# Operand tiles of a hybrid decoder block moved to multiples of 512 bytes, its feed-forward transposes spread over the next block, and w_down taken in halves between blocks of w_up

## The chip, the cores and the metric

The kernel runs on one core of a Trainium2 chip. The metric is the device time of one execution in microseconds (us), the median of several runs.

## The reference

One layer of a hybrid decoder block on 256 tokens of width 2048, in float32:

```python
u = rmsnorm(h, norm1_g);  proj = u @ w_in            # HGRN2 q,f,i,g; attention q,k,v; two gates
ya = hgrn2_branch(hq, hf, hi, hg) @ w_proj_a
yb = dilated_attention_branch(aq, ak, av) @ w_proj_b
h = h + (sigmoid(gate_a) * ya + sigmoid(gate_b) * yb) @ w_out
v = rmsnorm(h, norm2_g)
hup = v @ w_up                                       # 2048 x 11264
hc = depthwise causal conv of width 3 over tokens (hup) + conv_b
h = h + (gelu(hc[:, :5632]) * hc[:, 5632:]) @ w_down # 5632 x 2048
return rmsnorm(h, norm_f_g)
```

## The kernel before

All weights (318 MB) pass once through the core, in one stream of units. A unit is 128 x 2048 floats (1 MB): 16 tiles of 128 x 128. `load` (L230) issues its DMA on SP's queue into one of three `raw` buffers. `split` (L288) makes of each half a high part `hi` (a copy by ACT, L306, in the matmul's rounded type) and a low part `lo` (raw minus hi, by DVE, L311), in four buffers each. `begin_unit` (L344) splits two units ahead of the one that PE is at. A float32 product then is three products of PE: low operand with hi, high with hi, high with lo.

In a product the stationary operand is 128 x 128 and the moving one 128 x 512 (or x 256 in part of the first stage). `tile_step` (L374) takes the weights as the stationary operand and the tokens `xu` as the moving one (attention's q and k, HGRN2's q and f). `moving_step` (L459) takes the tokens as the stationary operand and the weights as the moving one: v and out-gate (names `avp`, `vp`, `gp`), gates (`egp`), `yb`, `ya`, `wo`, and w_down (`dn`).

For w_up, `sevenfold` (L508) takes two rows of blocks and two columns of blocks of the weights per unit, into seven banks of PSUM. A unit of mode P is eight block products (24 of PE); a unit of mode S (`split_s`, L262) is seven (21 of PE), with sums of weight blocks (`sa`, `se`, `sf`, `sg`) and sums of token blocks (`hvs`, `hvx`). Mode A is P with another way to the low part of its second half: ACT writes the negated raw (L308), and a DMA of POOL's queue adds raw to it (L309). A block b of w_up is eight units in the modes `SPAPSAPA`; there are eleven blocks. `unfold` (L524) combines the seven banks into four tiles, and `convolved` (L928) transposes them on PE (L936) into side banks and does the convolution with one ACT and two DVE instructions for each 128 columns (L939 to L941). Gelu, a multiplication and the split into `ff` follow. After blocks 3, 6, 9 and 11 (`PARTS`, L34) all of w_down's rows for these blocks pass, for each of four column blocks j. A scheduler sets the order of each engine's instructions from the order in which the program is traced and from the buffers.

Where the tiles lie follows from the pools, one behind the other in each partition. Counted modulo 512 bytes, the tiles of pools `wp` (raw, hi, lo, sa) and `sb` (tag `w4`: ot, ob, ff, hva, hvs, hvx) start at 448. Those of `sbe`, `sbm`, `sbh` and `sbl` (xu, mix, hvd, se, sf, sg) start at 480, since the small tiles at the end of `sb` shift what lies behind them. Every product operand starts at a multiple of 512 bytes within its tile.

Of the kernel before, what the change touches and what calls it, by code (L numbers as in the profile page):

```python
# [11 lines left out]
F32 = mybir.dt.float32  # L12
F32R = mybir.dt.float32r
# [29 lines left out]

START_X = {0: ((2, 4),), 1: ((4, 8),), 2: ((8, 12),), 3: ((12, 16),)}
# [1 line left out]

def up_order(b):

    return (1, 2, 0, 3, 5, 4, 6, 7) if b == 0 else tuple(range(KD // 2))

# [3 lines left out]
def stream_spec():  # L54
    spec, modes = [], {}

    def stat(name, col, k0, nk):
        for k in range(k0, k0 + nk):
            spec.append((name, k * P, col))

    def mov(name, col, k0, nk):
        for k in range(k0, k0 + nk):
            for c in range(4):
                spec.append((name, k * P, col + c * P))

    def pairs(name, n1, n2, k0, modes_of, order):

        for i in order:
            mode = modes_of[i]
            k2, k1 = k0 + 2 * i, k0 + 2 * i + 1  # L70
# [33 lines left out]
    for b0, b1 in PARTS:  # L104
        for b in range(b0, b1):
            pairs("w_up", b * 512, DFF + b * 512, 0, UP_PAIRS, up_order(b))
        for j in range(NJ):
# [59 lines left out]
def hybrid_block(ctx, tc, x_p, x_t, weights, g1, gf, params, c_rope, c_mask0, c_mask1, c_level, out):  # L167
    nc = tc.nc
    vec, act, pe = nc.vector, nc.scalar, nc.tensor

    const = ctx.enter_context(tc.tile_pool(name="const", bufs=1))
    wp = ctx.enter_context(tc.tile_pool(name="wp", bufs=1))
    sb = ctx.enter_context(tc.tile_pool(name="sb", bufs=1))
    early = ExitStack()
    sbe = early.enter_context(tc.tile_pool(name="sbe", bufs=1))
    psm = ctx.enter_context(tc.tile_pool(name="psm", bufs=4, space=bass.MemoryType.PSUM))
    pss = ctx.enter_context(tc.tile_pool(name="pss", bufs=4, space=bass.MemoryType.PSUM))

    def w4(shape, name, dt=F32):
        return sb.tile([P] + list(shape), dt, tag="w4", name=name, bufs=20)  # L180
# [81 lines left out]
    def split_s(u):  # L262
# [7 lines left out]
        q = pool.tile([P, 2, 512], F32, tag="q", name=f"q{u}", bufs=1)  # L270
# [6 lines left out]
        vec.tensor_tensor(r[:, 3], r[:, 3], r[:, 2], op=ALU.add)  # L277
# [5 lines left out]
        splits[u] = {  # L283
            "11": (ah[:, 0], al[:, 0]), "21": (ah[:, 1], al[:, 1]), "22": (eh[:, 0], el[:, 0]),
            "q3": (eh[:, 1], el[:, 1]), "q1": (fh[:, 0], fl[:, 0]), "q2": (fh[:, 1], fl[:, 1]), "q4": (g[:, 0], g[:, 1]),
        }

    def split(u):  # L288
# [8 lines left out]
        for s in range(2):  # L297
# [4 lines left out]
            for q in range(n):  # L302
# [1 line left out]
                if u < KD // 2 and q == 0:  # L304
                    split_x(2 * u + s)
                last[0] = act.activation(hi[:, q * w : (q + 1) * w], raw, AF.Copy)  # L306
                if s and MODES.get(u) == "A":
                    act.activation(lo, raw, AF.Copy, scale=-1.0)  # L308
                    nc.gpsimd.dma_start(lo, raw, accum_op=ALU.add)  # L309
                else:  # L310
                    last[1] = vec.tensor_tensor(lo[:, q * w : (q + 1) * w], raw, hi[:, q * w : (q + 1) * w].bitcast(F32), op=ALU.subtract)  # L311
            parts.append((hi, lo))
        splits[u] = parts

# [150 lines left out]
            pe.matmul(pst[m], xh, hi, start=False, stop=False)  # L465
            pe.matmul(pst[m], xh, lo, start=False, stop=(k == k0 + nk - 1))  # L466

    def moving(parts, k0, nk, name):

        pst = [main_bank(f"{name}_{m}") for m in range(2)]  # L470
        for k in range(k0, k0 + nk):
            moving_step(pst, parts, k, k0, nk)
        return pst
# [8 lines left out]
            (5, "a21", "12"), (5, "a22", "22"), (3, "d1", "12"), (3, "d2", "22"),  # L482
        ),
    }
    PRODUCTS["A"] = PRODUCTS["P"]

    def operands(a, mode, i, name):

# [18 lines left out]

    def sevenfold(ops, modes_of, order, name):  # L508

        banks = {i: (main_bank if i < 5 else side_bank)(f"{name}_{i}") for i in range(1, 8)}  # L510
        left = {i: sum(p[0] == i for mode in modes_of for p in PRODUCTS[mode]) for i in banks}
        fresh = set(banks)
        for i in order:
            w = next_pair()
            for b, x, n in PRODUCTS[modes_of[i]]:
                (xh, xl), (wh, wl) = ops[i][x], w[n]
                left[b] -= 1
                pe.matmul(banks[b], xl, wh, start=b in fresh, stop=False)  # L518
                pe.matmul(banks[b], xh, wh, start=False, stop=False)  # L519
                pe.matmul(banks[b], xh, wl, start=False, stop=left[b] == 0)  # L520
                fresh.discard(b)
        return banks

    def unfold(p, r, name):  # L524

# [396 lines left out]
    rstd2 = rsqrt_tokens(ss2, "rstd2")  # L922

    mid.close()
    late["pool"] = late["stage"] = ctx.enter_context(tc.tile_pool(name="sbl", bufs=1))


    def convolved(ups, c0, name):  # L928

        t = late["pool"].tile([P, FB, T], F32, tag="uc", name=f"{name}c", bufs=2)  # L930
        for i in range(2):
            pt = side_bank(f"{name}t{i}").rearrange("p (c t) -> p c t", c=2)
            for c in range(2):
                for m in range(2):
                    n = (2 * i + c) * P
# [1 line left out]
            for c in range(2):  # L937
# [1 line left out]
                act.activation(d, s, AF.Identity, bias=pc("cb", col), scale=pc("cw2", col))  # L939
                vec.scalar_tensor_tensor(d[:, 1:], s[:, : T - 1], pc("cw1", col), d[:, 1:], op0=ALU.mult, op1=ALU.add)  # L940
                vec.scalar_tensor_tensor(d[:, 2:], s[:, : T - 2], pc("cw0", col), d[:, 2:], op0=ALU.mult, op1=ALU.add)  # L941
        return t

    ss3 = square_sums("ss3")
    for part, (b0, b1) in enumerate(PARTS):
        ff = [w4([2, 2, T], f"ff{part}_{i}", F32R) for i in range((b1 - b0) * FB // 2)]
        for b in range(b0, b1):
            a0, a1, g0, g1_ = unfold(sevenfold(hv, UP_PAIRS, up_order(b), f"up{b}"), rstd2, f"up{b}")
            a = convolved((a0, a1), b * FB, f"ua{b}")
            gelu = act.activation(a, a, AF.Gelu_apprx_tanh)  # L950
            if b == NBLK - 1:

                with in_turn(gelu):
                    act.activation(small([1], "tab", "tab", 1), eps, AF.Sqrt)
            g = convolved((g0, g1_), NFF + b * FB, f"ub{b}")
            vec.tensor_tensor(g, a, g, op=ALU.mult)
            for i in range(2):
                d, s = ff[(b - b0) * 2 + i], g[:, 2 * i : 2 * i + 2]
                act.activation(d[:, :, 0], s, AF.Copy)
                vec.tensor_tensor(d[:, :, 1], s, d[:, :, 0].bitcast(F32), op=ALU.subtract)  # L960

        if b1 == NBLK:
            gfb = [w4([2, 512], f"gfb{i}") for i in range(2)]
            for i in range(2):
                nc.gpsimd.dma_start(gfb[i].rearrange("p a n -> p (a n)"), gf[:, i * 1024 : (i + 1) * 1024].to_broadcast([P, 1024]))

        def ff_parts(k, m, ff=ff, k0=b0 * FB):
            t = ff[(k - k0) // 2][:, (k - k0) % 2]
            return t[:, 0, m * P : (m + 1) * P], t[:, 1, m * P : (m + 1) * P]

        for j in range(NJ):
            pst = moving(ff_parts, b0 * FB, (b1 - b0) * FB, f"dn{part}_{j}")
# [62 lines left out]
```

## Time and profile before

| | |
|---|---|
| median of 3 runs | 1787.72 us (1786.76 to 1787.87) |
| profiled execution | 1786.24 us |
| span of its instructions | 1784.5 us |
| first stage up to w_out, from the first product | 6.4 to 1020.4 us of the span |
| w_up and w_down | 1020.4 to 1772.4 us |
| final norm and output | 1772.4 to 1784.5 us |

PE is TensorE, PEld its weight loads, DVE VectorE, ACT ScalarE, POOL GpSimd and SP SyncE. A matmul's row starts when its operand begins to stream, and ends when its modelled result is out, so that rows overlap: how fast PE goes is read from starts, or from how many products fall into a stretch. A row of a group reads: line, engine, operation, output<-inputs, shape, how many | busy us, mean ns of one | idle time before them and what ended it.

### The profile page before, as it was taken

The numbers are of one execution on the slowest core, as the hardware profiler recorded it, in microseconds if no ns is written. First come the engines' busy times: TensorE is split into PE (matmuls) and PEld (weight loads), VectorE is DVE, ScalarE is ACT, GpSimd is POOL, SyncE is SP. The second block draws the span as 40 slices with busy tenths as digits, with TensorE's granted clock in tenths as the row PEclk, the third lists the DMA queues.
The fourth block names the chain that finished last, engine by engine and source line by source line (L and its number), as shares of the span: only waits on it lengthen the run. The fifth ranks groups of instructions, "written<-read, shape, count | busy, mean of one in ns | idle before, by whom it ended". The sixth has DMA issues, their size and how long they took to land.

```text
span 1784.5 us, 21599 instructions
## 1 busy us (share of the span) xinstructions
PE 1754.5 (98%) x8406; PEld 1453.0 (81%) x8406; DVE 1204.1 (67%) x1499; ACT 951.7 (53%) x1177; POOL 38.3 (2%) x57
## 2 busy tenths in 40 slices
PE   9999999999999999999999999999999999999997
PEld 7888888888888888888887877888787887788775
DVE  7765675867768575445566588766786667776765
ACT  6444565545454545444445567555665456654653
POOL 0000000000000000000000000000000000000000
PEclk9999999999999999999999999999999999999998
DMA  7765644444544444556555576656666566655672
GB/s 271 236 212 201 211 143 154 167 167 166 180 167 169 164 167 160 184 187 236 184 183 189 174 237 212 199 204 206 200 219 214 190 216 224 205 212 201 213 232 85
DMA packets 53126, 345.35 MB, mean 194 GB/s; under 512 B 6128, under 2 KB 6384, under 8 KB 14880
## 3 DMA queue, kind: packets, MB, share of 16 engines
q1 hardware_dynamic: 45648, 318.28, 49.6%
q0 software_dynamic: 6224, 22.55, 6.1%
q10 hardware_dynamic: 1152, 3.15, 0.5%
q8 instruction: 66, 1.08, 0.2%
q14 instruction: 36, 0.29, 0.0%
HBM read 321.41 MB, written 2.10 MB: 181 GB/s over the span
## 4 chain that ended last, share of the span: by engine, by line
PE 89%; DVE 4%; DMA 4%; issue 2%; ACT 1%; SPq 0%; DVEq 0%; POOLq 0%; ACTq 0%
PE up L520 7%; PE up L519 7%; PE up L518 7%; PE dn L464 4%; PE dn L465 4%; PE dn L466 4%; PE egp L464 3%; PE egp L466 3%; PE egp L465 3%; DMA lo<-raw 3%; PE ak L377 2%; PE gp L464 2%; PE gp L466 2%; PE vp L464 2%; PE vp L466 2%
## 5 line engine op out<-in xcount | busy, mean ns | idle before, releaser
L306 ACT ACTIVATE hi<-raw 128x1024 fp32r<-128x1024 f32 (+1 forms) x558 | 588.0, 1056 | 703.1 <-PE dn L465 108.0
L311 DVE TENSOR_TENSOR lo<-raw,hi 128x1024 fp32r<-128x1024 f32 (+1 forms) x525 | 638.8, 1219 | 434.8 <-ACT hi L306 426.4
L520 PE MATMUL up<-lo,hva 128*128 128x512 f32 x396 | 155.5, 393 | 2.7 <-DMA lo<-raw 2.7
L518 PE MATMUL up<-hi,hva 128*128 128x512 f32 x396 | 154.7, 391 | 0.0
L519 PE MATMUL up<-hi,hva 128*128 128x512 f32 x396 | 154.6, 390 | 0.0
L464 PE MATMUL dn<-hi,ff 128*128 128x512 f32 x352 | 138.7, 395 | 2.9 <-DVE ff L960 2.9
L466 PE MATMUL dn<-lo,ff 128*128 128x512 f32 x352 | 137.0, 391 | 1.0 <-DVE lo L311 1.0
L465 PE MATMUL dn<-hi,ff 128*128 128x512 f32 x352 | 137.9, 392 | 0.0
L464 PE MATMUL egp<-hi,xu 128*128 128x512 f32 x256 | 102.1, 399 | 0.0
L466 PE MATMUL egp<-lo,xu 128*128 128x512 f32 x256 | 101.3, 396 | 0.0
L465 PE MATMUL egp<-hi,xu 128*128 128x512 f32 x256 | 101.2, 396 | 0.0
L520 PEld LDWEIGHTS up<-lo,hva 128*128 128x128 f32 x396 | 74.3, 188 | 21.4 <-DMA lo<-raw 5.7
L519 PEld LDWEIGHTS up<-hi,hva 128*128 128x128 f32 x396 | 74.3, 188 | 16.0
L518 PEld LDWEIGHTS up<-hi,hva 128*128 128x128 f32 x396 | 74.4, 188 | 15.9
L464 PEld LDWEIGHTS dn<-hi,ff 128*128 128x128 f32 x352 | 66.5, 189 | 17.7 <-DVE ff L960 4.2
L466 PEld LDWEIGHTS dn<-lo,ff 128*128 128x128 f32 x352 | 66.4, 189 | 15.3 <-DVE lo L311 1.5
L465 PEld LDWEIGHTS dn<-hi,ff 128*128 128x128 f32 x352 | 66.6, 189 | 13.3
L377 PE MATMUL ak<-xu,hi 128*128 128x512 f32 x192 | 66.7, 390 | 0.0
L309 POOL DMA_DIRECT2D lo<-raw x33 | 28.8, 872 | 1491.0 <-ACT lo L308 1360.4
L466 PEld LDWEIGHTS egp<-lo,xu 128*128 128x128 f32 x256 | 48.1, 188 | 11.6
L465 PEld LDWEIGHTS egp<-hi,xu 128*128 128x128 f32 x256 | 48.1, 188 | 11.2
L464 PEld LDWEIGHTS egp<-hi,xu 128*128 128x128 f32 x256 | 48.1, 188 | 11.1
(583 smaller groups left out, 3737.5 us busy)
## 6 DMA issues: line engine op xcount, KB each, us to landing
raw<-weights SPq DMA_DIRECT2D x298, 1024.0 KB, 4.8
lo<-raw POOLq DMA_DIRECT2D x33, 512.0 KB, 5.3
h<-x_t ACTq DMA_DIRECT2D x4, 512.0 KB, 4.5
xt<-x_p SPq DMA_DIRECT2D x3, 512.0 KB, 10.4
xs_q<-aqraw POOLq DMA_DIRECT2D x6, 256.0 KB, 6.6
xs_k<-akraw POOLq DMA_DIRECT2D x6, 256.0 KB, 7.6
raw<-weights SPq DMA_DIRECT2D x4, 256.0 KB, 4.5
raw<-weights SPq DMA_DIRECT2D x2, 512.0 KB, 7.4
```

The source lines that it names most:

```text
L306: last[0] = act.activation(hi[:, q * w : (q + 1) * w], raw, AF.Copy)
L309: nc.gpsimd.dma_start(lo, raw, accum_op=ALU.add)
L311: last[1] = vec.tensor_tensor(lo[:, q * w : (q + 1) * w], raw, hi[:, q * w : (q + 1) * w].bitcast(F32), op=ALU.subtract)
L377: pe.matmul(ps, hi, pair, start=(k == 0), stop=False, skip_group_check=True)
L464: pe.matmul(pst[m], xl, hi, start=(k == k0), stop=False)
L465: pe.matmul(pst[m], xh, hi, start=False, stop=False)
L466: pe.matmul(pst[m], xh, lo, start=False, stop=(k == k0 + nk - 1))
L518: pe.matmul(banks[b], xl, wh, start=b in fresh, stop=False)
L519: pe.matmul(banks[b], xh, wh, start=False, stop=False)
L520: pe.matmul(banks[b], xh, wl, start=False, stop=left[b] == 0)
```

## The change

Three edits.

**Places.** The small tiles get a pool of their own (`smp`) ahead of the others, followed by an unused tile of 136 floats. With it all tiles of `wp`, `sb`, `sbe`, `sbm`, `sbh` and `sbl` start at multiples of 512 bytes. `ones`, `ident` and the other constants stay where they were.

**w_up.** The modes of a block become `SPPSPPPP`: two S and six P as products go, but no A, so the three A halves of a block are split by ACT and DVE as the others are. `split_s` keeps its sums in `raw`'s own blocks, and q1, q2 and q4 change places in the tiles. The seven sums and the transposes get a fixed bank each (`late_bank`; 8 is the transposes').

**Side work.** `hidden_side` is a generator: unfold at the end of a block, then two empty steps, then the convolution's four groups of four transposes, gelu and the split into ff; `begin_unit` takes about one step at each following unit. w_down no longer passes in four parts: from block 2 on, after each block, two column blocks j of the two blocks before that are finished (`DOWN`), eight k tiles each.

```diff
-PARTS = ((0, 3), (3, 6), (6, 9), (9, NBLK))
-UP_PAIRS = "SPAPSAPA"
+DOWN = {b: [(j, b - 2 - b % 2, b - b % 2) for j in ((2, 3) if b % 2 else (0, 1))] for b in range(2, NBLK)}
+DOWN[NBLK - 1] += [(2, NBLK - 3, NBLK), (3, NBLK - 3, NBLK), (0, NBLK - 1, NBLK), (1, NBLK - 1, NBLK)]
+UP_PAIRS = "SPPSPPPP"
+HIDDEN_WAIT = 2
+ALIGN = 136
...
-    return (1, 2, 0, 3, 5, 4, 6, 7) if b == 0 else tuple(range(KD // 2))
+    return (1, 2, 0, 4, 3, 5, 6, 7) if b == 0 else tuple(range(KD // 2))
...
     const = ctx.enter_context(tc.tile_pool(name="const", bufs=1))
+    smp = ctx.enter_context(tc.tile_pool(name="smp", bufs=1))
+    align = ctx.enter_context(tc.tile_pool(name="align", bufs=1))
+    nc.gpsimd.memset(align.tile([P, ALIGN], F32, name="align"), 0.0)
     wp = ctx.enter_context(tc.tile_pool(name="wp", bufs=1))
...
-        return sb.tile([P] + list(shape), F32, tag=tag, name=name, bufs=bufs)
+        return smp.tile([P] + list(shape), F32, tag=tag, name=name, bufs=bufs)
...
-        vec.tensor_tensor(q[:, 0], r[:, 0], r[:, 3], op=ALU.add)
+        vec.tensor_tensor(q1, r[:, 0], r[:, 3], op=ALU.add)
         two_parts(ah, al, r[:, 0:2])
         vec.tensor_tensor(r[:, 3], r[:, 3], r[:, 2], op=ALU.add)
-        vec.tensor_tensor(q[:, 1], q[:, 0], r[:, 2], op=ALU.add)
+        vec.tensor_tensor(r[:, 0], q1, r[:, 2], op=ALU.add)
         two_parts(eh, el, r[:, 2:4])
-        vec.tensor_tensor(r[:, 0], q[:, 1], r[:, 1], op=ALU.add)
-        two_parts(fh, fl, q[:])
-        two_parts(g[:, 0], g[:, 1], r[:, 0])
+        vec.tensor_tensor(r[:, 1], r[:, 1], r[:, 0], op=ALU.add)
+        two_parts(fh, fl, r[:, 0:2])
+        two_parts(g[:, 0], g[:, 1], q1)
...
-                if s and MODES.get(u) == "A":
-                    act.activation(lo, raw, AF.Copy, scale=-1.0)
-                    nc.gpsimd.dma_start(lo, raw, accum_op=ALU.add)
-                else:
-                    last[1] = vec.tensor_tensor(lo[:, q * w : (q + 1) * w], raw, hi[:, q * w : (q + 1) * w].bitcast(F32), op=ALU.subtract)
+                last[1] = vec.tensor_tensor(lo[:, q * w : (q + 1) * w], raw, hi[:, q * w : (q + 1) * w].bitcast(F32), op=ALU.subtract)
...
+    def hidden_side(b, sums):
+        c11, c21, c12, c22 = unfold(sums, rstd2, f"up{b}")
+        for _ in range(HIDDEN_WAIT):
+            yield SIDE_US
+        a, g = (late["pool"].tile([P, FB, T], F32, tag="uc", name=f"u{n}{b}", bufs=2) for n in "ab")
+        yield from convolve((c11, c21), b * FB, a, f"ua{b}")
+        gelu = act.activation(a, a, AF.Gelu_apprx_tanh)
...
+        yield from convolve((c12, c22), NFF + b * FB, g, f"ub{b}")
+        vec.tensor_tensor(g, a, g, op=ALU.mult)
...
+    for b in range(NBLK):
+        sums = sevenfold(hv, UP_PAIRS, up_order(b), f"up{b}")
+        drain()
+        side.append(hidden_side(b, sums))
+        pump(0.0001)
+        for j, b0, b1 in DOWN.get(b, ()):
...
+            pst = moving(ff_parts, b0 * FB, (b1 - b0) * FB, f"dn{b}_{j}", [late_bank(i, f"dn{b}_{j}_{i}") for i in ((4, 3) if j % 2 else (1, 5))])
```

On PE, where block 0 of w_up ends and block 1 begins, before (`ua0t` takes the transposes of block 0's tiles `up0c`; `sah`, `sal` open block 1):

```order
L520 MATMUL up_3_8049<-lo_1_8251,hvd_8017 128x512
L936 MATMUL ua0t_8376<-ident,up0c_8362 128x128
L936 MATMUL ua0t_8387<-ident,up0c_8362 128x128
L518 MATMUL up_1_8427<-sah_8279,hvs_7469 128x512
L519 MATMUL up_1_8427<-sah_8279,hvs_7469 128x512
L520 MATMUL up_1_8427<-sal_8280,hvs_7469 128x512
L518 MATMUL up_2_8428<-sah_8279,hvs_7469 128x512
L519 MATMUL up_2_8428<-sah_8279,hvs_7469 128x512
L520 MATMUL up_2_8428<-sal_8280,hvs_7469 128x512
L518 MATMUL up_2_8428<-hi_0_8324,hva_7485 128x512
L936 MATMUL ua0t_8376<-ident,up0c_8363 128x128
L936 MATMUL ua0t_8376<-ident,up0c_8362 128x128
```

The same place with the change, from the last products of block 1's first unit (an S unit) on:

```order
L523 MATMUL up_5_8383<-sg_8289,hvx_7478 128x512
L521 MATMUL up_3_8381<-seh_8285,hvx_7478 128x512
L522 MATMUL up_3_8381<-seh_8285,hvx_7478 128x512
L523 MATMUL up_3_8381<-sel_8286,hvx_7478 128x512
L945 MATMUL ua0t_8441<-ident,up0c_8366 128x128
L945 MATMUL ua0t_8441<-ident,up0c_8367 128x128
L945 MATMUL ua0t_8441<-ident,up0c_8366 128x128
L945 MATMUL ua0t_8441<-ident,up0c_8367 128x128
L521 MATMUL up_2_8380<-hi_0_8328,hva_7493 128x512
L522 MATMUL up_2_8380<-hi_0_8328,hva_7493 128x512
```

Before, two transposes stand right behind the block's last product and the other fourteen seven products later; now the first four stand a whole unit, 21 products, behind it, and the other twelve in fours further on.

On DVE, after block 0's tiles (`up0c`) are made, before (`ua0c` and `ub0c` are the convolution's results, `lo` a weight unit's low part):

```order
L539 SCALAR_TENSOR_TENSOR up0c_8364<-up_3_8049,rstd_r,up0c_8364 128x512
L311 TENSOR_TENSOR lo_0_8435<-raw_8332,hi_0_8434 128x1024
L940 SCALAR_TENSOR_TENSOR ua0c<-ua0t_8376,par,ua0c 128x255
L940 SCALAR_TENSOR_TENSOR ua0c<-ua0t_8387,par,ua0c 128x255
L941 SCALAR_TENSOR_TENSOR ua0c<-ua0t_8376,par,ua0c 128x254
L941 SCALAR_TENSOR_TENSOR ua0c<-ua0t_8387,par,ua0c 128x254
L940 SCALAR_TENSOR_TENSOR ub0c<-ub0t_8400,par,ub0c 128x255
L940 SCALAR_TENSOR_TENSOR ub0c<-ub0t_8411,par,ub0c 128x255
```

And with the change (`q`, `sg`, `sel`, `sal` belong to the S unit that PE reaches two units later):

```order
L283 TENSOR_TENSOR q_8417<-raw_8394 128x512
L285 TENSOR_TENSOR raw_8394<-raw_8394 128x512
L949 SCALAR_TENSOR_TENSOR ua_8439<-ua0t_8441,par,ua_8439 128x255
L268 TENSOR_TENSOR sg_8424<-q_8417,sg_8424 128x512
L950 SCALAR_TENSOR_TENSOR ua_8439<-ua0t_8441,par,ua_8439 128x254
L268 TENSOR_TENSOR sel_8421<-raw_8394,seh_8420 128x1024
L949 SCALAR_TENSOR_TENSOR ua_8439<-ua0t_8441,par,ua_8439 128x255
L268 TENSOR_TENSOR sal_8419<-raw_8394,sah_8418 128x1024
L950 SCALAR_TENSOR_TENSOR ua_8439<-ua0t_8441,par,ua_8439 128x254
L286 TENSOR_TENSOR raw_8394<-q_8417,raw_8394 128x512
L288 TENSOR_TENSOR raw_8394<-raw_8394 128x512
```

Before, the convolution's instructions stand together; now they alternate with the preparation of the weights.

More of the change, by code (lines that the diff above doesn't have):

```diff
@@ L103, in stream_spec @@
         mov("w_out", j * 512, 0, KD)
[L104 to L107, printed above, removed]
+    for b in range(NBLK):
+        pairs("w_up", b * 512, DFF + b * 512, 0, UP_PAIRS, up_order(b))
+        for j, b0, b1 in DOWN.get(b, ()):
             mov("w_down", j * 512, b0 * FB, (b1 - b0) * FB)
@@ L466, in moving_step, with moving @@
             pe.matmul(pst[m], xh, lo, start=False, stop=(k == k0 + nk - 1))
-    def moving(parts, k0, nk, name):
-        pst = [main_bank(f"{name}_{m}") for m in range(2)]
+    def moving(parts, k0, nk, name, pst=None):
+        pst = pst or [main_bank(f"{name}_{m}") for m in range(2)]
         for k in range(k0, k0 + nk):
@@ L484, in hybrid_block @@
     }
-    PRODUCTS["A"] = PRODUCTS["P"]
     def operands(a, mode, i, name):
@@ L508, in sevenfold @@
     def sevenfold(ops, modes_of, order, name):
-        banks = {i: (main_bank if i < 5 else side_bank)(f"{name}_{i}") for i in range(1, 8)}
-        left = {i: sum(p[0] == i for mode in modes_of for p in PRODUCTS[mode]) for i in banks}
-        fresh = set(banks)
+        sums = {i: late_bank(i, f"{name}_{i}") for i in range(1, 8)}
+        left = {i: sum(p[0] == i for mode in modes_of for p in PRODUCTS[mode]) for i in sums}
+        fresh = set(sums)
         for i in order:
@@ L517, in sevenfold @@
                 left[b] -= 1
-                pe.matmul(banks[b], xl, wh, start=b in fresh, stop=False)
-                pe.matmul(banks[b], xh, wh, start=False, stop=False)
-                pe.matmul(banks[b], xh, wl, start=False, stop=left[b] == 0)
+                pe.matmul(sums[b], xl, wh, start=b in fresh, stop=False)
+                pe.matmul(sums[b], xh, wh, start=False, stop=False)
+                pe.matmul(sums[b], xh, wl, start=False, stop=left[b] == 0)
                 fresh.discard(b)
-        return banks
+        return sums
     def unfold(p, r, name):
@@ L924, in hybrid_block, with late_bank, convolve @@
     mid.close()
+    banks.close()
+    psu = ctx.enter_context(tc.tile_pool(name="psu", bufs=1, space=bass.MemoryType.PSUM))
+    def late_bank(i, name):
+        return psu.tile([P, 512], F32, tag=f"b{i}", name=name)
     late["pool"] = late["stage"] = ctx.enter_context(tc.tile_pool(name="sbl", bufs=1))
-    def convolved(ups, c0, name):
-        t = late["pool"].tile([P, FB, T], F32, tag="uc", name=f"{name}c", bufs=2)
+    def convolve(ups, c0, t, name):
         for i in range(2):
-            pt = side_bank(f"{name}t{i}").rearrange("p (c t) -> p c t", c=2)
+            pt = late_bank(8, f"{name}t{i}").rearrange("p (c t) -> p c t", c=2)
             for c in range(2):
@@ L941, in convolved @@
                 vec.scalar_tensor_tensor(d[:, 2:], s[:, : T - 2], pc("cw0", col), d[:, 2:], op0=ALU.mult, op1=ALU.add)
-        return t
-    ss3 = square_sums("ss3")
[L945 to L972, printed above, removed]
@@ new lines, in convolve @@
+            yield SIDE_US
+    ff = {}
+    def hidden_side(b, sums):
+        c11, c21, c12, c22 = unfold(sums, rstd2, f"up{b}")
+        for _ in range(HIDDEN_WAIT):
+            yield SIDE_US
+        a, g = (late["pool"].tile([P, FB, T], F32, tag="uc", name=f"u{n}{b}", bufs=2) for n in "ab")
+        yield from convolve((c11, c21), b * FB, a, f"ua{b}")
+        gelu = act.activation(a, a, AF.Gelu_apprx_tanh)
+        if b == NBLK - 1:
+            with in_turn(gelu):
+                act.activation(small([1], "tab", "tab", 1), eps, AF.Sqrt)
+        yield from convolve((c12, c22), NFF + b * FB, g, f"ub{b}")
+        vec.tensor_tensor(g, a, g, op=ALU.mult)
+        ff[b] = [w4([2, 2, T], f"ff{b}_{i}", F32R) for i in range(2)]
+        for i in range(2):
+            d, s = ff[b][i], g[:, 2 * i : 2 * i + 2]
+            two_parts(d[:, :, 0], d[:, :, 1], s)
@@ new lines, in ff_parts @@
+    def ff_parts(k, m):
+        t = ff[k // FB][k % FB // 2][:, k % 2]
+        return t[:, 0, m * P : (m + 1) * P], t[:, 1, m * P : (m + 1) * P]
+    gfb = []
+    ss3 = square_sums("ss3")
+    for b in range(NBLK):
+        sums = sevenfold(hv, UP_PAIRS, up_order(b), f"up{b}")
+        drain()
+        side.append(hidden_side(b, sums))
+        pump(0.0001)
+        for j, b0, b1 in DOWN.get(b, ()):
+            if b1 == NBLK and not gfb:
+                drain()
+                for i in range(2):
+                    gfb.append(w4([2, 512], f"gfb{i}"))
+                    nc.gpsimd.dma_start(gfb[i].rearrange("p a n -> p (a n)"), gf[:, i * 1024 : (i + 1) * 1024].to_broadcast([P, 1024]))
+            pst = moving(ff_parts, b0 * FB, (b1 - b0) * FB, f"dn{b}_{j}", [late_bank(i, f"dn{b}_{j}_{i}") for i in ((4, 3) if j % 2 else (1, 5))])
```

10 lines of the change are left out of this document (6 added, 4 removed).

## The prediction

> **What bounds the kernel now.** First the page: busy shares, and the chain of work that ended last.
>
> ```profile
> PE 1754.5 (98%) x8406; PEld 1453.0 (81%) x8406; DVE 1204.1 (67%) x1499; ACT 951.7 (53%) x1177; POOL 38.3 (2%) x57
> ...
> PE 89%; DVE 4%; DMA 4%; issue 2%; ACT 1%; SPq 0%; DVEq 0%; POOLq 0%; ACTq 0%
> ```
>
> PE is busy for 98% of the span and holds 89% of the chain. So two things can shorten it: products that follow each other faster, and waits of PE that go. How fast they follow is read from starts, in the view of one tile in a stretch without gaps (how many: shortest/median/longest ns, first and last start). Here w_in's gates, w_proj_a, w_down and attention's k:
>
> ```profile
> L464 PE MATMUL egp<-hi,xu x96: 395/396/396, 747.5 to 814.0; 128*128 128x512 f32 x96
> ...
> L464 PE MATMUL ya<-hi,ot x32: 389/389/389, 820.2 to 841.3; 128*128 128x512 f32 x32
> ...
> L464 PE MATMUL dn<-hi,ff x48: 389/389/389, 1192.0 to 1223.9; 128*128 128x512 f32 x48
> ...
> L377 PE MATMUL ak<-xu,hi x48: 390/390/390, 59.8 to 76.1; 128*128 128x512 f32 x48
> ```
>
> A row holds one product in three, so `egp` starts one every 66.5 us / (95 x 3) = 233.3 ns, and `ya` and `dn` together one every (21.1 + 31.9) / (31 x 3 + 47 x 3) = 226.5 ns. Same shape, same engine, no wait: 6.8 ns apart, as are the rows' durations (396 and 389). What differs is where the operands lie. In `ya` and `dn` both start at 448 modulo 512 (by the pools, above); in `egp` the stationary `xu` starts at 480. The same shows within single units of w_up, where one moving `hi` meets `hva` (448), then `hvd` (480):
>
> ```profile
> L519 PE MATMUL up<-hi,hva x30: 389/389/398, 1229.7 to 1260.0; 128*128 128x512 f32 x30
> ...
> L519 PE MATMUL up<-hi,hvd x10: 392/394/396, 1233.8 to 1261.4; 128*128 128x512 f32 x10
> ```
>
> 389 against 394, back and forth in each of ten units, so neither the stage nor other engines make it. `ak` is the exception: one operand at 480 (here the moving one), yet 390.
>
> Then the stretches of w_up and w_down: in all; block 1; the first w_down part; the end.
>
> ```profile
> core 0: us, PE busy (x) PEld busy (x) DVE busy (x) ACT busy (x) POOL busy (x), PEclk, DMA share, GB/s
> 1020.40:1772.40 752.00, 737.81 (x3287) 599.62 (x3285) 542.26 (x697) 436.45 (x532) 29.89 (x35) 1.00 0.62 204
> 1065.10:1111.10 46.00, 44.96 (x205) 36.40 (x204) 37.24 (x52) 31.75 (x39) 2.59 (x3) 1.00 0.68 220
> ...
> 1157.40:1224.60 67.20, 67.20 (x306) 55.54 (x305) 49.58 (x61) 33.44 (x38) 0.00 (x0) 1.00 0.56 204
> 1721.00:1772.40 51.40, 47.49 (x209) 38.36 (x207) 34.55 (x49) 24.59 (x38) 0.00 (x0) 0.97 0.32 121
> ```
>
> And who PE itself waited for:
>
> ```profile
> PE up L518 <- ACT hi L306: 3.2, 3, 1.2
> PE dn L464 <- DVE ff L960: 2.9, 1, 2.9
> PE up L520 <- DMA lo<-raw: 2.7, 5, 1.0
> ...
> PE ua0t L936 <- DVE up0c L538: 1.0, 1, 1.0
> ```
>
> Engines beside PE have room (DVE 542 of 752 us); the waits are single ones, at the edges of blocks.
>
> **The change part by part.** The sum is made against the profiled execution, 1786.24 us (span 1784.5 and 1.7 around it); the median shown is 1787.72, 1.5 more, which is added at the end.
>
> *Places, before w_up.* These products have their stationary operand at 480 (`xu`, or `mix` for `wo`):
>
> ```profile
> L465 PE MATMUL egp<-hi,xu 128*128 128x512 f32 x256 | 101.2, 396 | 0.0
> ...
> L465 PE MATMUL wo<-hi,mix 128*128 128x512 f32 x128 | 50.9, 398 | 0.0
> ...
> L465 PE MATMUL gp<-hi,xu 128*128 128x512 f32 x128 | 50.6, 396 | 0.0
> ...
> L465 PE MATMUL vp<-hi,xu 128*128 128x512 f32 x128 | 50.6, 395 | 0.0
> ...
> L465 PE MATMUL avp<-hi,xu 128*128 128x512 f32 x96 | 37.9, 395 | 0.0
> ```
>
> Three lines each: 3 x (256 + 128 + 128 + 128 + 96) = 2208 products. With both operands at multiples of 512 I take them to the faster of the two paces: 2208 x 6.8 ns = **15.0 us**. No row shows an operand at a multiple of 512. The nearest are the two paces: from above, nothing is gained (0); from below, the step from 480 to 448 comes once more (13.6 ns each). I take the pace that this trace shows. For `tile_step` (896 pairs like `ak`'s) the bounds are 0 and a step for each product, 896 x 2 x 6.8 = 12 us; I take 0, since its 390 is nearest to the 389.
>
> *w_up and w_down, as a sum.* The counts are these:
>
> ```profile
> L519 PE MATMUL up<-hi,hva 128*128 128x512 f32 x396 | 154.6, 390 | 0.0
> ...
> L464 PE MATMUL dn<-hi,ff 128*128 128x512 f32 x352 | 138.7, 395 | 2.9 <-DVE ff L960 2.9
> ...
> L519 PE MATMUL up<-hi,hvd 128*128 128x512 f32 x132 | 52.0, 394 | 0.0
> ...
> L519 PE MATMUL up<-sfh,hvx 128*128 128x512 f32 x44 | 17.4, 395 | 0.0
> L519 PE MATMUL up<-seh,hvx 128*128 128x512 f32 x44 | 17.3, 394 | 0.0
> L519 PE MATMUL up<-sah,hvs 128*128 128x512 f32 x44 | 17.3, 393 | 0.0
> ...
> L519 PE MATMUL up<-sg,hvs 128*128 128x512 f32 x22 | 8.7, 396 | 0.0
> ```
>
> Products: 3 x (396 + 132 + 44 + 44 + 44 + 22) + 3 x 352 = 3102, at 226.5 ns 702.6 us. Transposes: 176 (sixteen a block), priced by one group:
>
> ```profile
> L936 PE MATMUL ub0t<-ident,up0c x8: 272/273/276, 1068.7 to 1069.5; 128*128 128x128 f32 x8
> L939 ACT ACTIVATE ub0c<-ub0t,par x4: 548/562/568, 1069.5 to 1077.4; 128x256 f32<-128x256 f32 x4
> L940 DVE SCALAR_TENSOR_TENSOR ub0c<-ub0t,par,ub0c x4: 474/478/483, 1071.2 to 1078.0; 128x255 f32<-128x255 f32 x4
> ```
>
> Eight in 0.8 us, so 0.1 us each, 17.6 us, before as after. The stretch is 752.0 us; what is left, 752.0 - 702.6 - 17.6 = **31.8 us**, is lost time. It consists of: operands at 480 (`hvd` 396 and `se`, `sf`, `sg` 3 x 110 = 330), 726 x 6.8 = 4.9; the end, where block 10's results are waited for: 51.4 us hold 192 products (43.5) and fourteen transposes (1.4), so 6.5 lost; and the rest, 20.4, some 1.9 in each block (block 1: 46.0 - 186 x 0.2265 - 1.6 = 2.3), with the waits shown above in it.
>
> What goes of it: the 4.9 with the places. The 6.5, since w_down's pieces for blocks 8 and 9 (four units) and eight k tiles more come between block 10 and the first product that needs it: 24 k tiles x 6 x 0.2265 = 32.6 us of cover. And most of the 20.4: the transposes' wait for DVE (`up0c`), since a unit stands between; and the waits for the DMA that made the A units' low parts:
>
> ```profile
> lo<-raw POOLq DMA_DIRECT2D x33, 512.0 KB, 5.3
> ...
> SPq L237 <- DMA lo<-raw: 320.4, 33, 13.3
> ```
>
> SP's loads waited 320 us in all for that DMA to let `raw` go; now DVE's subtraction releases it, so DVE is late next. POOL's queue loses 33 DMAs, and nothing of it is moved elsewhere.
>
> What comes: DVE takes over 33 low parts, ACT loses 33 copies.
>
> ```profile
> L311 DVE TENSOR_TENSOR lo<-raw,hi 128x1024 fp32r<-128x1024 f32 (+1 forms) x525 | 638.8, 1219 | 434.8 <-ACT hi L306 426.4 <-PE lv L722 4.7 <-PE lv L746 1.6
> ...
> L308 ACT ACTIVATE lo<-raw 128x1024 fp32r<-128x1024 f32 x33 | 34.5, 1047 | 0.0
> ...
> L260 DVE TENSOR_TENSOR sfl<-q,sfh 128x1024 fp32r<-128x1024 f32 x22 | 26.8, 1219 | 3.6 <-ACT sfh L259 3.6
> ...
> L277 DVE TENSOR_TENSOR raw<-raw 128x512 f32<-128x512 f32 x22 | 15.1, 688 | 0.4
> ...
> L260 DVE TENSOR_TENSOR sg<-raw,sg 128x512 fp32r<-128x512 f32 x22 | 15.1, 684 | 0.4 <-ACT sg L259 0.4
> ```
>
> 33 x 1.22 = 40.3 us more for DVE, 34.5 less for ACT. DVE then has 542 + 40 = 583 of some 724 us, 80%, but in blocks 0 to 2, with no w_down between, 37.2 + 3.7 = 40.9 of 43.7 us, 94%. The cover is PE's own work; without it every microsecond goes to PE, so the bounds are 0 and 40 us. The trace shows DVE with 81% of block 1 and PE waiting some 2 us, which is far nearer to 0. I take **4 us** of waits that stay or are new (0.4 a block), and keep up to 15 in the range. The new order of S in a block and the longer way to `sfh` (now behind `sal` and two sums, some 1.2 + 2 x 0.69 us later) hide behind the two units, 10 us, that are split ahead.
>
> *At nothing.* The halves of w_down change banks, and 1 and 5 are written right after a block. The last reading of bank 5 is two instructions of DVE (0.74 each) after its sum, which ends six products (1.4 us) before the block does, and the piece's second bank is needed three products in. The memset, the small tiles' places, the start and the last 12 us stay as they are.
>
> Sum: 15.0 + 31.8 - 4 = **42.8 us**. 1786.24 - 42.8 = 1743.4, and with the 1.5 of the median **1745 us**.
>
> **The rivals.** *The step comes once more* (448 still costs): 2208 + 3102 products and `ya`'s 3 x 128, 5694 x 6.8 = 39 us, with `tile_step` 51: 1706 to 1694. For it: two paces are known, and no row says that 226.5 is the floor. Against it: `ak` does not follow the pattern, and nothing here was ever faster.
> [...]
>
> *DVE is late.* The 94% in the first blocks, and convolutions put between the weights' instructions, cost half of the 31.8 in place of 4: 12 us, 1757. For it: `lo` already waits 426 us for `hi` (its row above). Against it: w_down stands between the blocks from block 2 on.
>
> *The places do nothing*, and the paces differ for some other reason: 15.0 + 4.9 are not gained, 1765. Against it stand the ten units above.
> [...]
>
> *One bank for the transposes*, the case that ends slower: a group of four has to wait until DVE has read the group before (four of 0.48 and two of ACT's 0.56). Where the split of an S unit stands among them (3 x 1.22 + 5 x 0.69 = 7.1 us) that is 9.5 us for a unit of 5.4, and PE stands behind the transposes: 4.1 us in each of eleven blocks, 45 us, 1790. It decides from 3.9 us a block on. Against it: DVE's order puts the convolution's instructions between the split's, and the second group 25 products behind the first.
>
> **How the numbers follow.** Forecast 52% (1733 to 1756: 12 for `tile_step` below, 11 more waits above); the step again 20%; DVE late 12%; places without effect 9%; one bank 4%; something in between that ends near the time before 3%. The range, 1696 to 1768, takes in the forecast, DVE late, most of the step again and of the places without effect; it leaves out about 16%. A difference of 0.2% (3.6 us) is about what a measurement of this kernel can tell from none: faster 93%, within 3%, slower 4%.
>
> **What would show it.** `egp`, `vp`, `gp`, `avp` and `wo` at 389 ns, 96 products in 21.7 us and not 22.4; below 389, the step came again. `hvd` and `se` like `hva`. w_up and w_down in 724 us; no wait of several us at the end; blocks 1 and 2 near 44 us, longer if DVE is late, and then PE's waits name `lo` or the convolution's tiles. The forecast is wrong if `egp` stays at 396, if all rows fall below 389, or if the late stretch keeps over 740 us.

## The result, and the profile after

| | before | after |
|---|---|---|
| median | 1787.24 us (4 runs, 1784.72 to 1787.87) | 1755.18 us (4 runs, 1753.60 to 1756.18) |
| span of the profiled execution | 1784.5 us | 1754.4 us |

The ratio is 0.982 (95% interval 0.9805 to 0.9839), some 32 us faster. The forecast was 1745, so it was 10 us too low, inside its range.

The page of the changed kernel, its busy shares and its chain:

```profile
PE 1736.2 (99%) x8406; PEld 1451.5 (83%) x8406; DVE 1245.0 (71%) x1544; ACT 927.8 (53%) x1144; POOL 9.6 (1%) x25
...
PE 97%; DVE 1%; ACT 0%; DMA 0%; issue 0%; SPq 0%; DVEq 0%
```

PE's share of the chain went from 89% to 97%: what is left is products. DVE has 40.9 us more work (1204.1 to 1245.0) and ACT 23.9 less. The paces, in the view of one tile, for the stretches shown of before (how many: shortest/median/longest ns, first and last start):

```profile
L468 PE MATMUL egp<-hi,xu x65: 389/389/389, 741.2 to 784.7; 128*128 128x512 f32 x65
...
L468 PE MATMUL ya<-hi,ot x32: 389/389/389, 811.9 to 833.0; 128*128 128x512 f32 x32
...
L381 PE MATMUL ak<-xu,hi x50: 395/398/403, 58.8 to 76.1; 128*128 128x512 f32 x50
```

`egp` now goes as `ya` does: 43.5 us / (64 x 3) = 226.6 ns. `ya` has not moved, and no product is faster than it was. `ak` got slower: 17.3 us / 49 pairs = 353 ns a pair, where the kernel before had 17.3 / 50 = 346 ns:

```profile
L377 PE MATMUL ak<-xu,hi x51: 390/390/390, 58.8 to 76.1; 128*128 128x512 f32 x51
```

The late stretch of the changed kernel by windows, in all and for block 1:

```profile
core 0: us, PE busy (x) PEld busy (x) DVE busy (x) ACT busy (x) POOL busy (x), PEclk, DMA share, GB/s
1014.10:1742.70 728.60, 728.54 (x3278) 598.88 (x3278) 579.44 (x736) 408.68 (x492) 1.09 (x2) 1.00 0.51 186
1058.00:1102.40 44.40, 44.35 (x203) 36.33 (x202) 40.02 (x54) 29.32 (x36) 0.00 (x0) 1.00 0.50 186
```

PE's list of waits (us in total, times, longest):

```profile
PE up L521 <- ACT hg L921: 2.3, 1, 2.3
PE avp L468 <- ACT hi L314: 1.4, 1, 1.4
```

752.0 us became 728.6, block 1 44.4 where it was 46.0, and all waits inside w_up and at the end have gone from the list. DVE is busy for 90% of block 1, and none of PE's waits in w_up names it. But a new wait of 2.3 us, at the entry of w_up, heads the list. Against the forecast, by the first and last starts of the tiles (the last `wo` product at 1009.8, before 1020.2; the first `up` product at 1014.1, before 1020.4):

| stretch | forecast | measured |
|---|---|---|
| up to the last product of w_out | -15.0 | -10.4 |
| from there to the first product of w_up | 0 | +4.1 |
| w_up and w_down | -27.8 | -23.4 |
| tail | 0 | -0.4 |
| span | -42.8 | -30.1 |

### The profile page after: what moved, and what is told of

Read it like the earlier page. It is cut to its first block, busy times and chain, and to the rows that moved or that the text cites. A ratio compares the mean times of both kernels' runs of the same rounds, so it can differ in the third digit from the quotient of the medians.

```text
span 1754.4 us, 21472 instructions
## 1 busy us (share of the span) xinstructions
PE 1736.2 (99%) x8406; PEld 1451.5 (83%) x8406; DVE 1245.0 (71%) x1544; ACT 927.8 (53%) x1144; POOL 9.6 (1%) x25
## 4 chain that ended last, share of the span: by engine, by line
PE 97%; DVE 1%; ACT 0%; DMA 0%; issue 0%; SPq 0%; DVEq 0%
PE up L523 9%; PE up L522 9%; PE up L521 9%; PE dn L468 5%; PE dn L470 5%; PE dn L469 5%; PE egp L470 3%; PE egp L469 3%; PE egp L468 3%; PE ak L381 3%; PE aq L381 2%; PE gp L468 2%; PE gp L469 2%; PE gp L470 2%; PE ya L470 2%; PE ya L469 2%
## 5 line engine op out<-in xcount | busy, mean ns | idle before, releaser
L315 DVE TENSOR_TENSOR lo<-raw,hi 128x1024 fp32r<-128x1024 f32 (+1 forms) x558 | 678.5, 1219 | 413.4 <-ACT hi L314 405.2
L469 PEld LDWEIGHTS dn<-hi,ff 128*128 128x128 f32 x352 | 66.1, 188 | 13.4
L382 PE MATMUL ak<-xu,lo 128*128 128x256 f32 x192 | 53.9, 281 | 0.0
```

The costliest lines, as they stand in the source:

```text
L382: pe.matmul(ps[:, T:], lo, pair[:, :T], start=False, stop=(k == nk - 1), skip_group_check=True)
```

## The experiments

All times are medians; the kernel before ran beside them with medians of 1785.7 to 1786.2 us. Each comparison is with that.

**The places and the rest apart (e1, e2).** e1 is the kernel before with the new pool:

```diff
+    smp = ctx.enter_context(tc.tile_pool(name="smp", bufs=1))
+    align = ctx.enter_context(tc.tile_pool(name="align", bufs=1))
+    nc.gpsimd.memset(align.tile([P, ALIGN], F32, name="align"), 0.0)
...
-        return sb.tile([P] + list(shape), F32, tag=tag, name=name, bufs=bufs)
+        return smp.tile([P] + list(shape), F32, tag=tag, name=name, bufs=bufs)
```

> The kernel before with the operands at multiples of 512 bytes alone (small tiles in a pool ahead, the filling tile); order, halves and modes stay as before. Theory (an operand at 480 costs 6.8 ns a product): 15.0 us before w_up and 4.9 in w_up go, egp, gp, vp, avp and wo fall from 396 to 389 ns, hvd from 394 to 389; and since the pairs of tile_step got slower in the changed kernel (ak 390 to 399 ns), some 3 us come back if that too is the places' doing: 1787 - 17 = 1770 us. Rival (the paces differ for another reason than the places): 1787 and egp at 396. If ak stays at 390 here, the slower pairs of the changed kernel come from its order, and the time is 1767.

Measured: 1773.78 us, ratio 0.993 (0.9918 to 0.9942), 12 us instead of 17. `egp` is at 389 and `ak` at 398, so the slower pairs come with the places. From the last product of w_out to the end of the span nothing was gained (764.0 us, before 764.3); the waits grew where the products got faster:

```profile
PE up L525 <- DMA lo<-raw: 5.0, 7, 1.0
PE up L523 <- ACT hi L311: 3.0, 3, 1.1
...
DVE q L280 <- DMA raw<-weights: 43.0, 11, 5.9
```

(before: 2.7, 3.2, and 40.8 in DVE's row). e2 is the changed kernel without those lines.

> The changed kernel without the places: small tiles back among the large ones, no filling tile, so operands at 448 and 480 as before; the spread convolution, the halves and the modes stay. Theory: egp at 396 and ak at 390 as before the change, and the time is that of the changed kernel plus 17 (19.9 for the products, less some 3 for the pairs): 1772 us, that is 15 under the kernel before, where the prediction had 22.9 for this part. If the two halves of the change help or hinder each other, the time and e1's do not add up: the sum of both gains is then not 32 us. Rival (places do nothing): 1755.

Measured: 1772.28 us, ratio 0.9923 (0.9909 to 0.9936), as expected. The two parts alone give 12 and 13.4 us, together 32: the faster products of w_up were worth something here only when the weights came in time (in e1 the late stretch is 0.3 us shorter).

**Which places count (e3 to e6).** Only the fillers differ from the changed kernel. e3 has the first line below; e5 has 128 there; e4 keeps 136 and has the other two lines ahead of the pool `sbe`; e6 has 128, and the two lines ahead of `sb`.

```diff
-ALIGN = 136
+ALIGN = 120
...
+    pad = ctx.enter_context(tc.tile_pool(name="pad", bufs=1))
+    nc.gpsimd.memset(pad.tile([P, 8], F32, name="pad"), 0.0)
```

> The changed kernel with a filling tile 64 bytes shorter: every operand starts at 448 modulo 512 and none at a multiple of 512. Theory (a multiple of 64 is enough, and 480 cost because it is none): same time as the changed kernel, 1755 us within 0.2%, egp and hvd at 389. Rival (multiples of 512 are what counts): products at 396 again, 2208 x 6.8 + 4.9 = 20 us more, 1775. For ak: 399 if both operands at the same place is what slows the pairs, 390 if a start at 512 does.

> The changed kernel with 32 bytes put ahead of the early pool and of the late ones that follow it, so that xu, mix, hvd and the se, sf, sg tiles start at 32 modulo 512, and hi, lo, hva and ff stay at multiples of 512. Theory: egp, vp, gp, avp, wo back at 396, hvd at 394, but ak (xu moves there, hi is stationary) at 390 and its pairs at 346.7 ns: 1755 + 19.9 - 3 = 1772. Rival (what slows the pairs is no matter of places): ak stays at 399, 1775. Second rival (32 is as good as 0, and only 480 was bad): 1755 with egp at 389.

> The changed kernel with the filling tile 32 bytes shorter, so that all operands of products start at 480 modulo 512, equal to each other and none at a multiple of 64. Theory A (a stationary operand at 480 costs 6.8 ns wherever the moving one lies): the products of w_out's kind, w_up and w_down and the gates, 2208 + 3102 + 384, all at 396 ns and 233.3 ns apart: 1755 + 5694 x 6.8 = 1794 us, and ya, dn and hva leave 389 for the first time. Theory B (what costs is that the two operands lie differently): 1755, egp at 389 and ak at 399 as in the changed kernel.

> The changed kernel with the split weights' pool alone at 480 modulo 512: hi, lo, sah, sal start there and xu, mix, hva, hvd, ff and the se, sf, sg tiles at multiples of 512. So the moving operand of egp, wo, ya, dn and most of up is at 480 and the stationary one at 0, and in tile_step it is the other way round. Theory A (the stationary operand's place sets the 6.8 ns): egp, ya, dn and hva stay at 389; tile_step's first product, with hi stationary at 480, stays at 399 or gets longer. Its bounds: 1755 and 1755 + 896 x 2 x 6.8 = 1767. Theory B (two operands that lie differently cost it): 5694 products at 396, 1794, and ak at 390.

Measured: e3 1757.05, e4 1770.79, e5 1756.36, e6 1783.99 us. In e3 the rows stay as in the changed kernel (`egp` 389, `ak` 398); in e4 `egp` is back at 396 and `ak` at 390. Tile rows of e5 (all at 480), then of e6 (the weights at 480, the rest at 0):

```profile
L468 PE MATMUL egp<-hi,xu x65: 389/389/389, 740.8 to 784.3; 128*128 128x512 f32 x65
...
L381 PE MATMUL ak<-xu,hi x51: 395/398/403, 58.6 to 76.2; 128*128 128x512 f32 x51
```

```profile
L471 PE MATMUL egp<-hi,xu x64: 395/396/396, 740.8 to 784.9; 128*128 128x512 f32 x64
...
L470 PE MATMUL ya<-hi,ot x21: 395/396/396, 820.3 to 834.3; 128*128 128x512 f32 x21
...
L383 PE MATMUL ak<-xu,hi x52: 390/390/390, 58.5 to 76.2; 128*128 128x512 f32 x52
```

With everything at 480 the products are as fast as with everything at 512. With the stationary operands at 0 and the weights that move at 480 they are slow, `ya` for the first time. So in these runs neither 480 nor 512 matters, nor which of the two operands is off: the 6.8 ns (396 against 389) are there where the two starts, counted modulo 512, lie 32 bytes apart (448 and 480, 0 and 32, or 480 and 0 across the end), and not where they are the same. Other distances were not run. Attention's pairs in `tile_step` (`ak`) take 346 to 347 ns at that distance (before, e4, e6) and 352 to 353 at the same start (the changed kernel, e5). Theory B of e5 and e6 holds; theory A falls, and so do the multiples of 512 and of 64. In e6 theory B's time, 1794, is 10 us above the measured one: its count had 330 products of S units whose operands still agree (2.2 us), the pairs got faster (2.2), and the rest was not followed up.

**The entry of w_up (e7).** One pool of banks from the start:

```diff
-    psm = banks.enter_context(tc.tile_pool(name="psm", bufs=4, space=bass.MemoryType.PSUM))
-    pss = banks.enter_context(tc.tile_pool(name="pss", bufs=4, space=bass.MemoryType.PSUM))
+    psu = ctx.enter_context(tc.tile_pool(name="psu", bufs=1, space=bass.MemoryType.PSUM))
+    def next_bank(first, name):
+        turn[first] += 1
+        return psu.tile([P, 512], F32, tag=f"b{first + (turn[first] - 1) % 4}", name=name)
...
-    banks.close()
-    psu = ctx.enter_context(tc.tile_pool(name="psu", bufs=1, space=bass.MemoryType.PSUM))
```

> The changed kernel with one pool of eight named banks from the start, in place of two pools that are closed ahead of w_up; the late banks' names and order stay. Theory: the wait at the entry of w_up (2.6 us behind w_out's last transposes, then some nine products at 427 ns with the granted clock at 0.51, 1.9 us) comes from the closed pools, which put all of ht3's transposes ahead of up0's first product; with them inside up0 again it goes, and wo3 and up0 together fall from 70.8 us to some 66: 1755 - 4.5 = 1750.5. Rival (the wait is for the weights' split or for ss2's chain, and no matter of the pools): 1755, the same wait in another place.

The place in the changed kernel, in the timeline of PE (start, length, engine, line), then in windows (third from the end is the granted clock):

```profile
1009.77 0.39 PE L470 MATMUL wo<-lo,mix 128*128 128x512 f32 x1
1010.26 0.44 PE L918 MATMUL ht<-ident,h 128*128 128x128 f32 x2
1010.94 0.87 PE L918 MATMUL ht<-ident,h 128*128 128x128 f32 x6 [0.24 <-DVE h L912]
1014.11 0.50 PE L521 MATMUL up<-hi,hva 128*128 128x512 f32 x1 [2.30 <-ACT hg L921]
...
1015.23 0.63 PE L521 MATMUL up<-hi,hva 128*128 128x512 f32 x1
1015.65 0.63 PE L522 MATMUL up<-hi,hva 128*128 128x512 f32 x1
```

```profile
1011.50:1014.10 2.60, 0.31 (x3) 0.07 (x1) 2.25 (x5) 2.52 (x7) 0.00 (x0) 1.00 0.36 50
1014.10:1017.90 3.80, 3.79 (x10) 2.97 (x11) 2.94 (x7) 2.15 (x6) 0.00 (x0) 0.55 0.57 241
1017.90:1021.90 4.00, 4.00 (x19) 3.29 (x18) 2.25 (x4) 3.35 (x4) 0.00 (x0) 1.00 0.00 0
```

All eight transposes of `ht` stand ahead of `up`, PE waits 2.3 us, and then starts a product every 0.42 us instead of every 0.227, with a granted clock of 0.55 over 3.8 us. The same place in e7:

```profile
1010.60:1013.00 2.40, 2.40 (x16) 1.84 (x15) 2.10 (x4) 1.86 (x4) 0.00 (x0) 1.00 0.36 150
1013.00:1016.00 3.00, 3.00 (x14) 2.17 (x13) 2.24 (x5) 3.00 (x7) 0.00 (x0) 1.00 0.76 216
```

No idle time, and a granted clock of 1.00. Measured: 1752.50 us, ratio 0.9814 (0.9801 to 0.9828), 2.7 us under the changed kernel's median. Of the profiled executions the span is 3.9 us shorter (1750.5, and 1754.4 in the changed kernel, the longest of its four). The closed pools made the wait. In the changed kernel's profiled execution the granted clock behind it was 0.55 over 3.8 us, and 0.45 of 3.8 us is 1.7 us lost.

**What the late gain is made of (e8, e9, e10).** e8 is e1 with the new modes, e9 is e1 with the low parts alone, e10 the changed kernel with the old modes. The edit of e9; e8 has `"SPPSPPPP"` and the changed kernel's `up_order` with it, and e10 takes the same lines back in the changed kernel, with `"SPAPSAPA"`:

```diff
-                if s and MODES.get(u) == "A":
-                    act.activation(lo, raw, AF.Copy, scale=-1.0)
-                    nc.gpsimd.dma_start(lo, raw, accum_op=ALU.add)
-                else:
-                    last[1] = vec.tensor_tensor(lo[:, q * w : (q + 1) * w], raw, hi[:, q * w : (q + 1) * w].bitcast(F32), op=ALU.subtract)
+                last[1] = vec.tensor_tensor(lo[:, q * w : (q + 1) * w], raw, hi[:, q * w : (q + 1) * w].bitcast(F32), op=ALU.subtract)
...
-UP_PAIRS = "SPAPSAPA"
+UP_PAIRS = "SPPPSPPP"
```

> e1 (places alone) with the modes of the changed kernel: no low part by DMA, all by DVE, S units at 0 and 3; w_down in four parts and the convolution undivided as before. Theory (in e1 the 4.9 us that faster products of w_up give were lost in waits for the DMA's low parts and for hi, which grew from 5.9 to 8.0 us): these waits go and those for the convolution (up0c and so on) stay: 1774 - 6 = 1768, w_up's block 1 at 45. Rival (DVE has no room without the spreading): waits for lo and for the convolution's tiles grow, 1774 or over.

> e1 with one thing more: the low parts of the A units by DVE and not by DMA; S stays at units 0 and 4, w_down in four parts, the convolution undivided. Theory (the DMA held raw, so the S unit's weights came late, DVE stood idle 43 us for them, in ten or eleven blocks, and the unfolding behind it came late to PE): DVE's wait q <- raw<-weights goes, and the whole gain of e8 is there: 1756. Rival (it is S at unit 3 in place of 4, which lies better between the blocks): 1765 or over, and DVE still waits some 40 us for the S unit's weights.

> The changed kernel with its modes put back: A units with low parts by DMA at 2, 3, 6 and 7 of S at 0 and 4; places, spread convolution and halves of w_down stay. Theory (spreading and halves save the 6 us at the end and cost 4.5 at the entry, and the DMA's cost comes back nearly whole): e1's 1774 less 1.5, 1772. Rival (the spread convolution moves the unfolding out of the late S unit's way, so that the modes matter only without it): 1757.

Measured: e8 1755.84, e9 1756.30 (ratio 0.9833 both, 0.9819 to 0.9846 for e9), e10 1775.88 (0.9941, 0.9927 to 0.9954). All that e9 adds to e1 is that DVE makes the low parts, and it has the whole time of the changed kernel, 17.5 us under e1, with the convolution undivided and w_down in four parts. The changed kernel with the DMA back is as slow as e1. What PE and DVE waited for in e9, then in e10:

```profile
PE dn L465 <- DVE ff L961: 2.9, 1, 2.9
...
PE dn L467 <- DVE lo L312: 1.0, 1, 1.0
...
DVE q L280 <- DMA raw<-weights: 6.6, 5, 2.4
```

```profile
PE up L528 <- DMA lo<-raw: 14.7, 8, 2.3
PE up L526 <- ACT hg L926: 2.6, 1, 2.6
...
DVE q L283 <- DMA raw<-weights: 4.8, 6, 1.6
```

In e9 every wait of the block edges is gone (`up0c` and its like, `hi`, `lo<-raw`), though none of them but the last names the DMA; block 10's wait at the end is left, and 1.0 us for a `lo` in w_down. In e1 DVE stood idle for 43.0 us before the first sum of an S unit, for weights; with the low parts on DVE, 6.6. In e10 DVE's wait is small too, and PE waits for the DMA itself, 14.7 us. Neither number of e8's expectation came: it had taken only the waits that name the DMA or `hi`, and left those for the convolution standing.

**A version that ends below both (e11, e12).** e8 with w_down's end cut in another way, e11 by the first of the new lines and e12 by the second; the last two parts pass behind up10 (a second list, not shown, says which blocks of w_up pass ahead of each part):

```diff
-PARTS = ((0, 3), (3, 6), (6, 9), (9, NBLK))
+PARTS = ((0, 3), (3, 6), (6, 8), (8, 10), (10, NBLK))
+PARTS = ((0, 3), (3, 6), (6, 9), (9, 10), (10, NBLK))
```

> e8 (places, modes, undivided convolution) with w_down in five parts, blocks 0-2, 3-5, 6-7, then 8-9 and 10 by itself, these last two behind up10: 43 us of products of blocks 8 and 9 stand between up10 and the first product that reads block 10. e8's first product of the second piece behind up10 waited 2.9 us for ff, and that piece took 22.3 us for 16.3 of products. Theory: these 6 us go, and nothing comes for them: 1750. Rival (the wait at the end gives way to another, for weights or for DVE's sums, eight more of 0.68 us): 1755.

e11 missed: 1756.88 us. The wait was not gone but moved:

```profile
PE dn L466 <- DVE ff L963: 2.9, 1, 2.9
...
PE dn L468 <- DVE lo L313: 1.0, 1, 1.0
```

These are e9's rows again, now in the part of blocks 6 and 7, whose first block covers only 5.4 us of each piece.

> e8 again, w_down in the old parts of three blocks, and only the last part divided: blocks 0-2, 3-5, 6-8, then behind up10 block 9 alone for all four column blocks, and then block 10. e11's miss is the ground: a part of two blocks waits for its second block wherever it stands (dn2 there took 23.6 us for 16.3 of products), a part of three does not. In e8 block 10's results were there some 18.5 us behind up10 (7.1 of the first piece, 5.4 of the next, and 6 of waiting); here 4 x 5.44 + 1.4 = 23.2 us of other work stand there. Theory: the 6 us go, 1756 - 6 = 1750. Rival (pieces of half the length, eight in place of four, leave DVE's sums and the freeing of banks in the way, or the tail grows): 1755.

e12 came out as expected: 1751.15 us (1749.32 to 1751.35), ratio 0.9804 (0.9791 to 0.9817). What follows up10, for e8 and then for e12:

```profile
1690.80:1742.20 51.40, 47.46 (x209) 38.37 (x207) 34.67 (x49) 24.53 (x38) 0.00 (x0) 0.97 0.25 89
```

```profile
1691.40:1738.00 46.60, 45.63 (x209) 37.29 (x206) 39.80 (x58) 24.82 (x39) 0.00 (x0) 1.00 0.28 98
```

The same products take 4.8 us less. Some 1.5 us of it is the granted clock (0.97 over 51.4 us in e8, 1.00 in e12): in e9, with the same wait of 2.9 us but a granted clock of 1.00, these products take 49.9 us.

```profile
1691.10:1741.00 49.90, 46.00 (x209) 37.27 (x207) 34.65 (x49) 24.58 (x38) 0.00 (x0) 1.00 0.25 92
```

The five runs of e12 lie below all of the changed kernel's, but the two intervals against the kernel before overlap. e7's edit isn't in it and does not apply, since its pools are never closed.

## Why the prediction was right, and where it was not

**The size and the sign** were right, and so was what bounds the kernel. The 10 us that it was off, and the reasons that were wrong, are these.

**Places before w_up: 15.0 forecast, 10.4 measured.** The step per product was right: all rows named fell from 396 to 389. Two things were not. The step that priced `tile_step` at 0 with bounds of 0 and -12 left out a loss, on the ground that 390 was nearest to 389; its 390 with one operand at 480 was the advantage that the change took away. For attention's `ak` and `aq` that is (192 + 128) x 7 ns = 2.2 us; HGRN2's pairs hardly changed (64 of `z1p` went from 24.7 to 24.8 us). Of the other 2.4 us 0.5 is a first product that came later (at 6.9 us, before 6.4), and the rest is in small pieces that no run took apart. And the reason given, that an operand at 480 costs, was wrong, and it is luck that it gave the same sum here: with both at 480 (e5) `egp` takes 389 ns, with 0 and 480 (e6) 396. The kernel before could not tell the two apart, since each of its slow products had one operand at 448 and the other at 480; `ak`, with the same two places, was the row that spoke against a simple rule.

**w_up and w_down: 27.8 forecast, 23.4 measured.** The 4.9 us of the places are there, but only with the feed mended: e1 gained nothing in w_up, the changed kernel 5 against e2. The 6.5 at the end went as said: nothing waits for `ff` any more, and e12 finds the same wait worth 4.7 us. Some 1.5 of the 6.5 was a lower granted clock behind the wait (0.52 from 1738.0 to 1741.4): the prediction's row of the end shows 0.97 over 51.4 us, and its reason did not name it. The 20.4 at the block edges mostly went too, but not for the reason given, first of all the unit between transposes and DVE. In e9 these waits go though the order is the old one, and e10, with the new order, waits 14.7 us for the DMA: it was the low parts by DMA. The prediction had shown the row of SP's 320 us for `lo<-raw` and used it as a second reason; it had not looked at what DVE waited for, where this row of the kernel before says it:

```profile
DVE q L275 <- DMA raw<-weights: 40.8, 10, 5.5
```

DVE's idle time for the S units' weights was as long as the 40.3 us of work that it then took over; so *DVE is late* did not happen, though DVE is busy for 90% of block 1. Since both reasons led to the same 20.4, the sum held, by luck as far as the order of work was the reason. That the held `raw` is the link from the DMA to DVE's wait is read from the waits; it was not tested apart from the DMA's own traffic, nor from ACT's 33 copies (34.5 us) that go with it.

**The 4 us of waits that stay or come** is the term that was mis-sized. The same sum over the late stretch, 728.6 - 702.6 - 17.6, leaves 8.4 us. 1.7 of it are the granted clock of 0.55 behind the entry. Some 2 are estimated for the groups of four transposes: the one below takes 0.45 us and not the 0.4 of the price (1357.21 to 1358.11 is 0.90 us, with two products of 0.227 in it), and there are 44 groups. The other 4.7 are in smaller pieces that were not taken apart.

```profile
1357.21 0.39 PE L469 MATMUL dn<-hi,ff 128*128 128x512 f32 x1
1357.44 0.60 PE L945 MATMUL ua5t<-ident,up5c 128*128 128x128 f32 x4
1357.80 0.48 PE L470 MATMUL dn<-lo,ff 128*128 128x512 f32 x1
1358.11 0.40 PE L468 MATMUL dn<-hi,ff 128*128 128x512 f32 x1
```

**The entry: 0 forecast, 4.1 measured.** "At nothing" named the halves' banks and the start, but not the line that closes the two pools ahead of w_up. It moves all transposes of `ht3` ahead of the first product (some 0.9 us that were inside w_up before) and makes PE wait. The order of the changed kernel showed this place; the prediction had looked at the block edges alone.

**The rivals.** The step did not come once more: `egp` and `ya` start a product every 226.6 ns in the changed kernel, where `ya` and `dn` had 226.5 before. The places do something (`egp` 389 in e1, 396 in e4 and e6). One bank for the transposes costs no wait: none of PE's rows after names the convolution.

## What to carry to other kernels

Before a wait of PE is put down to the order of work, look at what the engine that it names was itself waiting for; here the waits named the unfolding on DVE, and the cause was the making of low parts by DMA, two steps up, which cost 17.5 us (e1 against e9). Look at where the two operands of a product start, and measure each kind of product with the same start and with another: here `egp` took 389 ns with the same start modulo 512 and 396 with starts 32 bytes apart, attention's `ak` 398 and 390 (whether a smaller modulus is enough was not tested). When pools are closed and opened between stages, look at the order of the instructions across that place; here PE waited 2.3 us there, and not in e7.

## What was not expected of the hardware

In these runs `moving_step`'s products of 128x512 started every 226.6 ns when the two operands' starts were the same modulo 512 (`egp` in the changed kernel at 0 and in e5 at 480; before, `ya` and `dn` at 448, 226.5) and every 233.3 ns when they lay 32 bytes apart (`egp` before, and in e4 and e6), whichever was off. A pair of attention's `tile_step` took 352 to 353 ns with the same start (the changed kernel, e5) and 346 to 347 with starts 32 bytes apart (before, e4, e6). Other distances were not tried.

Behind PE's wait of 2.30 us at the entry of w_up the granted clock of the changed kernel's profiled execution was 0.55 over 3.8 us: 0.50 from 1015.0 to 1017.5, with starts 0.42 to 0.43 us apart, and 1.00 again from 1018.0.

The length of the wait did not decide alone. e5 has the same wait of 2.30 us at the same place (in the first row, up to 1015.00), and the granted clock stays at 1.00 behind it:

```profile
1012.40:1015.00 2.60, 0.30 (x4) 0.07 (x2) 2.25 (x5) 2.53 (x7) 0.00 (x0) 1.00 0.29 50
1015.00:1018.80 3.80, 3.80 (x17) 3.14 (x18) 2.92 (x7) 3.12 (x7) 0.00 (x0) 1.00 0.57 241
```

Around the 2.9 us of e9 it is 1.00 too (over 49.9 us, above); around e8's 2.9 us it is 0.97 over 51.4 us. What decides was not tested, so the 1.7 us is the price in one execution and not in each.
